# Output projection of a decoder layer: seven block products in place of eight for six heads and 1024 columns, with x and the deeper weight ring moved

## The chip, the cores and the metric

The kernel runs on one NeuronCore of one Trainium2 chip. The metric is the device time of one execution in microseconds; the median of 3 runs is 1096.73 us (1096.45 to 1097.01). The engines are named TensorE (PE; PEld for its weight loads), VectorE (DVE), ScalarE (ACT), GpSimd (POOL) and SyncE (SP, which only issues DMAs here).

## The reference, cut to what matters

One layer of a hybrid decoder: 256 tokens, width 2048, everything in float32. The change is in one matrix product, that of the mixed heads with `w_out`, between the attention and the residual:

```python
h = rms_norm(x, ln_mix_pre[l])
proj = h @ w_in[l]
...
attn = moba_attention(q.reshape(shp), k.reshape(shp), v.reshape(shp), rel_bias)
ssm = mamba2_mixer(z, xbc, dt_raw, ...)
mixed = jnp.concatenate([attn, ssm], axis=-1) @ w_out[l]
x = x + rms_norm(mixed, ln_mix_post[l])
h = rms_norm(x, ln_ffn_pre[l])
u = causal_depthwise_conv(h @ w_ffn_up[l], ffn_conv_w[l], ffn_conv_b[l])
gate, up = jnp.split(u, [FFN_HIDDEN], axis=-1)
f = (jax.nn.gelu(gate, approximate=True) * up) @ w_ffn_down[l]
x = x + rms_norm(f, ln_ffn_post[l])
```

`attn` has 8 heads of 128 columns, `ssm` 1024 columns; so `w_out` is 2048 x 2048.

## The kernel before

**Products in three matmuls.** Both operands of a large product are split into a rounded value and a remainder (`whi` and `wlo` for weights, two parts of each activation). A product is high by high, high by low and low by high, three matmuls into one accumulator in PSUM. `rows_part` (L312 to L319) does that for one unit of weights and one half of the tokens: the activations are the stationary side, 512 columns of weights move.

**Units and the ring.** Weights come as units of 128 x 1024 float32 (512 KB), in the order of the list given to `Weights`. For each unit SP issues a DMA into `raw` (L85), ScalarE casts it to `whi` (L86) and VectorE subtracts to get `wlo` (L87). `take()` hands the next finished unit to TensorE's code; `tick()`, called behind the matmuls of each unit, fetches one unit more and runs what `defer(n, ...)` has put off by n ticks. There are 4 buffers of `raw` and 4 of `whi` and `wlo`, so unit n + 4 is cast when unit n has been multiplied. `deepen` (L75) adds three buffers to `whi` and `wlo` from a pool of its own, and lets three ticks fetch a second unit. Each engine runs its instructions in a fixed order, and a waiting instruction holds all that stand behind it on its engine.

**The output projection.** A unit here is 256 rows of `w_out` by 512 columns, so it takes 2 halves of tokens x 2 blocks of rows x 3 = 12 matmuls. Chunk c is columns 512 c to 512 c + 511. `mT` holds the operand, transposed: blocks 0 to 7 are the heads, 8 to 15 the `ssm` part. Before the last attention head is finished the `ssm` rows of chunks 0 and 1 are multiplied (`rows_chunk(first[c], mT, lo, last=False)`, 8 units), then the heads' rows of both chunks (`hi`, 8 units), then chunks 2 and 3 with all rows. The last head's own steps (`logits`, `transposed`, `values`) are deferred by ticks into the first units.

**Behind each chunk.** `post(c)` (L847) squares and sums the chunk on ScalarE from PSUM, and VectorE multiplies it by `wpost` (the post norm's row, L850) into `mm` and that by `lnrow` (L842, `weighted`). `x_weighted` (L845) multiplies 512 columns of x by `lnrow`. Accumulators of a chunk come from a pool of four (`acc`), which the two first chunks fill.

**The loads.** When the attention's memory is free, GpSimd issues four DMAs of 1 MB: x by rows (`xt`, two of them, L821), then `wpost` (L826) and `lnrow` (L829), each a row repeated on all partitions; ScalarE multiplies `wpost` by -0.5 (L827). The ring is deepened at the same place (L823).

**Seven products for eight.** The down projection of the feed-forward part already forms products of 2 x 2 blocks with seven block products (a quad). Two units are loaded for it (`same` and `other`), two more are made of them (`two` and `more`): `quad_step` casts each on ScalarE (L137), forms the sums on VectorE (L141, L144, L145) and the remainders (L146). Four units carry 7 products of 3 matmuls (`product`, L1091); `quad_operands` forms the activations' sums, and `quad_sums` puts the four shared accumulators together with `fa`. That part runs with the deepened ring.

Of the kernel before, what the change touches and what calls it, by code (L numbers as in the profile page):

```python
# [19 lines left out]
P = 128  # L20
D = 2048
# [43 lines left out]
class Weights:  # L65
# [89 lines left out]
    def take(self):  # L155
        while not self.ready:
            self.fetch()
        return self.ready.pop(0)


@with_exitstack
def decoder_layer(ctx, tc, x, xT, win, wdt, wout, wup, wdown, relb, vec, cols, mconv, fconv,
# [20 lines left out]
    def tok(t):  # L183
        return slice(t * P, (t + 1) * P)
# [137 lines left out]
    def rows_chunk(pss, aT, kts, first=True, last=True, done=None, soon=None):  # L322
# [11 lines left out]
        if done:  # L334
            for t in range(NT):
                done(t, pss[t])

    def rows_to_tail(pss, aT, kts, first=True):
# [15 lines left out]
    def down_units(half):  # L354

        found, at = [], half * 44
        for what in 2 * ORDERS[half]:
# [3 lines left out]
            else:  # L361
                found += units(wdown, at, 1)
                at += 1
        return found

    ws = Weights(nc, wp, units(win, 0, 16, SHIFT) + units(win, 16, 16) + units(win, 32, 16, SHIFT)
                 + units(win, 48, 16) + units(win, 64, 24, SHIFT) + units(wout, 0, 32)
                 + [u for half in range(2) for u in units(wup, half * 88, 88) + down_units(half)])
# [42 lines left out]
    with ExitStack() as mctx:  # L411
        mx = mctx.enter_context(tc.tile_pool(name="mx", bufs=1))
        mT = mx.tile([P, KT, 2, S], F32R, name="mT")

        with ExitStack() as actx:
# [369 lines left out]
            def values(h, pT):  # L785
                po = psum("pav")
                nc.tensor.matmul(po[:, :S], v[:, 0, tok(h)], pT[:, :S], start=True, stop=False)
                nc.tensor.matmul(po[:, :P], v[:, 1, tok(h)], pT[:, S:], start=False, stop=True)
                split_evac(mT, h, slice(0, S), po[:, S - 1::-1])

            def head(h):
# [26 lines left out]
        mm = pers.tile([P, NT, D], F32, name="mm", tag="mm", bufs=1)  # L818
        xt = pers.tile([P, NT, D], F32, name="xt", tag="xt", bufs=1)
        for t in range(NT):  # L820
            aux(out=xt[:, t, :], in_=x[0, tok(t), :])  # L821
# [25 lines left out]
        def post(c):  # L847
            def fn(t, ps):
                square_sum(ss[0][t][:, c:c + 1], ps)
                nc.vector.tensor_tensor(mm[:, t, chunk(c)], ps, wpost[:, chunk(c)], op=ALU.mult)  # L850
                weighted(t, c)
                if (t, c) == (1, 2):
                    x_weighted(t, c)
            return fn
# [41 lines left out]


        for i, (t, c) in enumerate(((0, 0), (1, 0), (0, 1), (1, 1), (0, 2), (1, 3))):
# [168 lines left out]

    def blocks(ap):
        return ap.rearrange("p (b c) -> p b c", c=P)

    g8 = [None]

    def quad_operands(k, cg, cu):
# [9 lines left out]
        nc.vector.tensor_tensor(v[:, 2:4], blocks(cg), blocks(cu), op=ALU.mult)  # L1083
        nc.vector.tensor_tensor(v[:, 4:8:2], v[:, 0:2], v[:, 3::-3], op=ALU.subtract)
        nc.vector.tensor_tensor(v[:, 5], v[:, 4], v[:, 1], op=ALU.subtract)
        nc.vector.tensor_tensor(v[:, 7], v[:, 2], v[:, 5], op=ALU.add)
        src, hi, lo = g8[0][:, P:], gx[:, j, 0, :], gx[:, j, 1, :]
        nc.scalar.copy(hi, src)
        nc.vector.tensor_tensor(lo, src, f32(hi), op=ALU.subtract)

    def product(ps, j, block, w, h, first, last):  # L1091

        a, b = (gx[:, j, c, :][:, tok(block)] for c in range(2))
        s = chunk(h)
        nc.tensor.matmul(ps, a, w[0][:, s], start=first, stop=False)  # L1095
        nc.tensor.matmul(ps, a, w[1][:, s], start=False, stop=False)  # L1096
        end[0] = nc.tensor.matmul(ps, b, w[0][:, s], start=False, stop=last).ins  # L1097

    def quad_sums(half, c, p1, p6, p7, q5):
# [3 lines left out]
        if half == 0:  # L1103
            nc.scalar.copy(f[0][0], p1)
            tt(f[1][0], p6, f[0][0], op=ALU.add)
            tt(f[0][1], p7, f[1][0], op=ALU.add)
            tt(f[1][1], q5, f[0][1], op=ALU.subtract)
            tt(f[1][0], q5, f[1][0], op=ALU.subtract)
            return
# [286 lines left out]
```

## Time and profile before

| what | value |
|---|---|
| median of 3 runs | 1096.73 us |
| the profiled execution, its own time | 1097.02 us |
| its span, first to last instruction | 1095.2 us |
| mean granted clock of TensorE | 0.999 |
| busy: TensorE, VectorE, ScalarE, GpSimd | 99%, 81%, 57%, 1% |
| HBM read, written | 214.44 MB, 2.11 MB |
| output projection's matmuls on TensorE | 277.4 to 368 us |

A row of a group reads: line, engine, operation, output and inputs (buffer numbers left out), shapes and count; then busy us and mean ns of one; then idle time ahead of it and what ended it. A row of a time line starts with its start in us from the span's start and its length; two rows that follow overlap somewhat, since operations are pipelined, so the distance of starts is what an engine needs for one. A row of waits is engine and line, the one waited for, then us in total, times, and the longest.

### The profile page before, as it was taken

Reading aid. Unit: us, or ns where it says so; the run is one execution under the profiler, and the core shown is the slowest. Engines: PE = TensorE matmul, PEld = TensorE weight load, DVE = VectorE, ACT = ScalarE, POOL = GpSimd, SP = SyncE. Lnnn points to the kernel's source line nnn. Section 1 sums busy time; section 2 is a strip of 40 time slices with the busy share of each in tenths; the row PEclk is TensorE's granted clock in tenths of the full one; section 3 lists DMA queues with packets and bytes.
Section 4 is the critical chain, followed back from the end, with each engine's and each line's share of the span. In section 5 each row is a group of like instructions: output and inputs, shape, how many; then the busy total and the mean of one; then the engine's idle time right before and its main releaser. Section 6 shows DMA issues by size and latency. Waiting matters only on the chain.

```text
span 1095.2 us, 15949 instructions
## 1 busy us (share of the span) xinstructions
PE 1089.5 (99%) x5858; PEld 936.1 (85%) x5858; DVE 885.4 (81%) x1422; ACT 622.8 (57%) x945; POOL 14.5 (1%) x24
## 2 busy tenths in 40 slices
PE   9999999999999999999999999999999999999998
PEld 7888888888888998888888888888888888888887
DVE  6689976766568699888878999978888787888987
ACT  6666544644455486655555564646556555565552
POOL 0000000000000000000000000000000000000000
PEclk9999999999999999999999999999999999999999
DMA  9858544554687276656665476675566665656562
GB/s 308 301 174 269 191 154 152 177 180 166 182 320 252 76 254 212 208 183 192 190 191 191 135 232 190 215 245 186 187 189 193 189 192 193 189 178 217 185 219 88
DMA packets 61646, 217.59 MB, mean 199 GB/s; under 512 B 7104, under 2 KB 8912, under 8 KB 60928
## 3 DMA queue, kind: packets, MB, share of 16 engines
q1 hardware_dynamic: 59616, 207.53, 58.5%
q0 software_dynamic: 1664, 8.59, 2.1%
q8 instruction: 46, 0.75, 0.3%
q10 hardware_dynamic: 288, 0.46, 0.1%
q14 instruction: 32, 0.26, 0.1%
HBM read 214.44 MB, written 2.11 MB: 198 GB/s over the span
## 4 chain that ended last, share of the span: by engine, by line
PE 99%; DMA 0%; SPq 0%; ACT 0%; DVE 0%; issue 0%
PE pa L253 37%; PE pa L254 19%; PE pa L317 5%; PE pa L319 5%; PE pa L318 5%; PE ph L318 4%; PE ph L317 4%; PE ph L319 4%; PE pa L1096 1%; PE pa L1097 1%; PE pa L1095 1%; PE pab L253 1%; PE ph L1096 1%; PE ph L1097 1%; PE ph L1095 1%; PE pa L262 1%
## 5 line engine op out<-in xcount | busy, mean ns | idle before, releaser
L86 ACT CAST whi<-raw 128x1024 fp32r<-128x1024 f32 (+2 forms) x353 | 365.2, 1038 | 323.0 <-PE pa L253 186.6
L87 DVE TENSOR_TENSOR wlo<-raw,whi 128x1024 fp32r<-128x1024 f32 (+2 forms) x353 | 424.7, 1208 | 141.6 <-ACT whi L86 133.6
L253 PE MATMUL pa<-h,whi 128*128 128x512 f32 x1360 | 471.7, 394 | 0.0
L254 PE MATMUL pa<-h,wlo 128*128 128x256 f32 x1360 | 379.2, 279 | 0.0
L253 PEld LDWEIGHTS pa<-h,whi 128*128 128x128 f32 x1360 | 255.4, 188 | 57.5
L254 PEld LDWEIGHTS pa<-h,wlo 128*128 128x128 f32 x1360 | 255.3, 188 | 0.0
L253 PE MATMUL pa<-hT,whi 128*128 128x512 f32 x384 | 137.0, 398 | 0.0
L254 PE MATMUL pa<-hT,wlo 128*128 128x256 f32 x384 | 107.2, 280 | 0.0
L253 PEld LDWEIGHTS pa<-hT,whi 128*128 128x128 f32 x384 | 72.1, 188 | 15.8 <-issue 0.2
L1034 DVE SCALAR_TENSOR_TENSOR cfc<-cfu,fcv,cfc 128x255 f32<-128x255 f32 (+1 forms) x176 | 83.4, 479 | 2.1 <-ACT cfc L1032 0.6
L317 PE MATMUL ph<-whi,gT 128*128 128x512 f32 x190 | 73.9, 389 | 0.0
L319 PE MATMUL ph<-whi,gT 128*128 128x512 f32 x190 | 73.9, 389 | 0.0
L318 PE MATMUL ph<-wlo,gT 128*128 128x512 f32 x190 | 73.9, 389 | 0.0
L254 PEld LDWEIGHTS pa<-hT,wlo 128*128 128x128 f32 x384 | 72.2, 188 | 0.4 <-issue 0.2
L137 ACT CAST whi<-ts 128x1024 fp32r<-128x1024 f32 x36 | 37.3, 1049 | 31.3 <-DVE ts L145 16.8
L1032 ACT ACTIVATE cfc<-cfu,fcv 128x256 f32<-128x256 f32 x88 | 52.2, 598 | 3.7 <-DVE cfu L1031 3.7
L317 PE MATMUL pa<-whi,hT 128*128 128x512 f32 x128 | 51.1, 399 | 0.0
L317 PE MATMUL pa<-whi,mT 128*128 128x512 f32 x128 | 50.3, 393 | 0.0
L319 PE MATMUL pa<-whi,hT 128*128 128x512 f32 x128 | 50.1, 391 | 0.0
L318 PE MATMUL pa<-wlo,hT 128*128 128x512 f32 x128 | 50.0, 391 | 0.0
L318 PE MATMUL pa<-wlo,mT 128*128 128x512 f32 x128 | 50.0, 390 | 0.0
L319 PE MATMUL pa<-whi,mT 128*128 128x512 f32 x128 | 49.9, 390 | 0.0
(306 smaller groups left out, 1391.2 us busy)
## 6 DMA issues: line engine op xcount, KB each, us to landing
raw<-in_wup_dram SPq DMA_DIRECT2D x176, 512.0 KB, 3.5
raw<-in_wdown_dram SPq DMA_DIRECT2D x88, 512.0 KB, 3.9
raw<-in_win_dram SPq DMA_DIRECT2D x85, 512.0 KB, 3.6
raw<-in_wout_dram SPq DMA_DIRECT2D x32, 512.0 KB, 4.0
xsq<-in_x_dram SPq DMA_DIRECT2D x4, 512.0 KB, 8.6
rows<-acd POOLq DMA_DIRECT2D x4, 512.0 KB, 8.0
xt<-in_x_dram POOLq DMA_DIRECT2D x2, 1024.0 KB, 7.2
xr<-in_xT_dram SPq DMA_DIRECT2D x6, 256.0 KB, 6.0
```

The costliest lines, as they stand in the source:

```text
L86: nc.scalar.copy(hi[:, s], raw[:, s])
L87: return lambda: nc.vector.tensor_tensor(lo[:, s], raw[:, s], f32(hi[:, s]), op=ALU.subtract)
L137: nc.scalar.copy(hi[:, :n], raw[:, :n])
L253: nc.tensor.matmul(ps, w[0][:, s], both, start=(k == 0), stop=False)
L254: end[0] = nc.tensor.matmul(ps[:, c], w[1][:, s], hi, start=False, stop=(k == KT - 1)).ins
L317: nc.tensor.matmul(ps, a, w[0][:, s], start=(first and j == 0), stop=False)
L318: nc.tensor.matmul(ps, a, w[1][:, s], start=False, stop=False)
L319: end[0] = nc.tensor.matmul(ps, b, w[0][:, s], start=False, stop=(last and j == 1)).ins
L1032: nc.scalar.activation(c, u, AF.Identity, scale=wv[:, 2:3], bias=wv[:, 3:4])
L1034: nc.vector.scalar_tensor_tensor(c[:, sh:], u[:, :S - sh], wv[:, 2 - sh:3 - sh], c[:, sh:], op0=ALU.mult, op1=ALU.add)
L1095: nc.tensor.matmul(ps, a, w[0][:, s], start=first, stop=False)
L1096: nc.tensor.matmul(ps, a, w[1][:, s], start=False, stop=False)
```

## The change

For heads 0 to 5 (three pairs) and chunks 0 and 1 together, the output projection is formed with quads. The string `OUTER` sets the order: a digit is a plain unit of that chunk, Q a quad of four units. The first six plain units run as before while the last head is finished; then come Q 1 Q 1 Q 0 1. Heads 6 and 7 and the `ssm` rows stay plain.

```diff
+OUTER = "000011Q1Q1Q01"
+OQ = OUTER.count("Q")
...
+class Spare:
+    def tile(self, *args, **kwargs):
+        self.n += 1
+        return self.places[self.n % len(self.places)]
...
                 split_evac(mT, h, slice(0, S), po[:, S - 1::-1])
+                if h < 2 * OQ:
+                    out_operands(h, po[:, S - 1::-1])
...
+            def out_operands(h, a):
+                j, odd = divmod(h, 2)
+                if not odd:
+                    og[0] = ax.tile([P, 8 * P], F32, name="og", tag="og", bufs=1)
+                    nc.scalar.copy(blocks(og[0])[:, 1::-1], blocks(a))
+                    return
+                nc.scalar.copy(blocks(og[0])[:, 2:4], blocks(a))
+                block_sums(blocks(og[0]))
+                split(oq[:, j, 0, :], oq[:, j, 1, :], og[0][:, 4 * P:])
...
+            mm = pers.tile([P, NT, D], F32, name="mm", tag="mm", bufs=1)
+            ws.sums = Spare([mm[:, t, UE:] for t in range(NT)])
             first = [chunk_psums() for _ in range(2)]
-            for c in range(2):
-                rows_chunk(first[c], mT, lo, last=False)
+            taken = [list(lo) + list(hi[OQ:]) for _ in range(2)]
+            for what in OUTER[:6]:
+                c = int(what)
+                rows_step(first[c], mT, taken[c].pop(0), first=len(taken[c]) == 4 - OQ + 3)
...
-        for t in range(NT):
-            aux(out=xt[:, t, :], in_=x[0, tok(t), :])
-        ws.deepen(ctx.enter_context(tc.tile_pool(name="wq", bufs=1, side="right")))
+        defer(21, ws.deepen, ctx.enter_context(tc.tile_pool(name="wq", bufs=1, side="right")))
...
         def post(c):
             def fn(t, ps):
+                m = mm[:, t, chunk(c)]
+                if c < 2:
+                    nc.vector.tensor_tensor(m, ps, m, op=ALU.add)
+                    ps = m
                 square_sum(ss[0][t][:, c:c + 1], ps)
...
+                if c < 2:
+                    defer(3 + c + t, rest)
...
+        def out_pair():
+            once = [psum("pm7") for _ in range(4)]
+            p1, p7, q5, p6 = once
+            j = 0
+            for what in OUTER[6:]:
+                if what == "Q":
+                    for items in (((p1, 0, 0), (first[1][0], 6, 1)), ((first[0][0], 1, 0),),
+                                  ((q5, 3, 0), (p7, 5, 1)), ((p6, 4, 0), (first[0][1], 2, 1))):
+                        w = ws.take()
+                        for ps, block, h in items:
+                            mine = any(ps is z for z in once)
+                            out_product(ps, j, block, w, h, mine and j == 0,
+                                        mine and j == OQ - 1)
+                        tick()
+                    j += 1
+                    if j == OQ:
+                        with tc.issue_after(end[0]):
+                            for t in range(NT):
+                                aux(out=xt[:, t, :], in_=x[0, tok(t), :])
+                        first_sums([[mm[:, t, chunk(n)] for t in range(NT)] for n in range(2)],
+                                   p1, p6, p7, q5)
...
-            defer(9 + i, x_weighted, t, c)
-        for c in range(2):
-            rows_chunk(first[c], mT, hi, first=False, soon=post(c))
+            defer(19 + i, x_weighted, t, c)
+        out_pair()
```

`rows_step` is one plain unit as `rows_chunk` has it; `block_sums`, `split`, `product_of` and `first_sums` are the bodies of what the down projection did in place (`first_sums` is a copy and four sums or differences of 512 columns). Sums of weights go to the second half of `mm`, which nothing uses yet. Four accumulators more (`pm7`) hold the shared products; `post` adds them to chunks 0 and 1 ahead of the squares.

How this moves instructions is shown at three places. First GpSimd, where the loads stand. Before:

```order
L194 TENSOR_TENSOR rsy<-rsa,mhalf 128x1 x4
L821 DMA xt<-in_x_dram 128x2048 x2
L826 DMA wpost<-in_vec_dram 128x2048
L829 DMA lnrow<-in_vec_dram 128x2048
L219 TENSOR_TENSOR lsy<-lsa,mhalf 128x1 x2
```

In the change, with the semaphores that each waits for:

```order
L207 TENSOR_TENSOR rsy<-rsa,mhalf 128x1 [waits DVE_49] x4
L909 DMA wpost<-in_vec_dram 128x2048 [waits DVE_49,DMAHW0_49,PE_49,Activation_49]
L912 DMA lnrow<-in_vec_dram 128x2048
L1020 DMA xt<-in_x_dram 128x2048 [waits DMASW5_49]
L1020 DMA xt<-in_x_dram 128x2048 [waits DMASW1_49]
L232 TENSOR_TENSOR lsy<-lsa,mhalf 128x1 [waits DVE_49] x2
```

The two loads of x stand behind the two rows of the norms instead of ahead of them; they wait for two DMAs of GpSimd's own queue (the earlier loads of the bias and of `rows`) and for no other engine.

Second VectorE, behind the values of the last head (`mT<-pav`). Numbers are those of the buffers; before, each `raw` is one unit:

```order
L87 TENSOR_TENSOR wlo_2977<-raw_2975,whi_2976 128x1024
L241 TENSOR_TENSOR mT_98<-pav_2981,mT_98 128x256
L87 TENSOR_TENSOR wlo_3069<-raw_3067,whi_3068 128x1024
L87 TENSOR_TENSOR wlo_3000<-raw_2998,whi_2999 128x1024
L87 TENSOR_TENSOR wlo_3075<-raw_3073,whi_3074 128x1024
```

In the change; raw_3062 and raw_3074 are the two blocks of the second quad, raw_3124 and raw_3136 those of the third (units 16 and 17), whi_3052 is unit 10 and whi_3114 unit 15:

```order
L254 TENSOR_TENSOR mT_98<-pav_3006,mT_98 128x256
L146 TENSOR_TENSOR mm_2862<-mm_2862,raw_3062 128x512
L89 TENSOR_TENSOR wlo_3053<-raw_3051,whi_3052 128x1024
L148 TENSOR_TENSOR wlo_3061<-raw_3062,whi_3060 128x1024
L148 TENSOR_TENSOR wlo_3073<-raw_3074,whi_3072 128x512
L147 TENSOR_TENSOR mm_2862<-mm_2862,raw_3074 128x512
L148 TENSOR_TENSOR wlo_3086<-mm_2862,whi_3085 128x1024
L148 TENSOR_TENSOR wlo_3104<-mm_2862,whi_3103 128x1024
L143 TENSOR_TENSOR mm_2862<-raw_3124,raw_3136 128x1024
L89 TENSOR_TENSOR wlo_3115<-raw_3113,whi_3114 128x1024
L148 TENSOR_TENSOR wlo_3123<-raw_3124,whi_3122 128x1024
L148 TENSOR_TENSOR wlo_3135<-raw_3136,whi_3134 128x512
```

Where one remainder followed the other in the order of the units, the sums for a quad now stand between them, and the sum of the third quad's two blocks (L143) stands ahead of the remainder of unit 15.

Third VectorE at the end of chunks 0 and 1. Before:

```order
L87 TENSOR_TENSOR wlo_3117<-raw_3115,whi_3116 128x1024
L845 TENSOR_TENSOR xl0_3044<-xt_3025,lnrow_3041 128x512
L87 TENSOR_TENSOR wlo_3123<-raw_3121,whi_3122 128x1024
L850 TENSOR_TENSOR mm_3024<-pa_2837,wpost_3038 128x512
L850 TENSOR_TENSOR mm_3024<-pa_2838,wpost_3038 128x512
L842 TENSOR_TENSOR ml0_3043<-mm_3024,lnrow_3041 128x512
```

In the change, from the last remainder of the third quad (unit 19) on; `pm7` are the shared products, `pa` the chunks' own accumulators:

```order
L148 TENSOR_TENSOR wlo_3166<-mm_2862,whi_3165 128x1024
L89 TENSOR_TENSOR wlo_3177<-raw_3175,whi_3176 128x1024
L89 TENSOR_TENSOR wlo_3186<-raw_3184,whi_3185 128x1024
L89 TENSOR_TENSOR wlo_3198<-raw_3196,whi_3197 128x1024
L89 TENSOR_TENSOR wlo_3210<-raw_3208,whi_3209 128x1024
L388 TENSOR_TENSOR mm_2862<-pm7_3044,mm_2862 128x512
L928 TENSOR_TENSOR xl0_3030<-xt_3013,lnrow_3027 128x512
L389 TENSOR_TENSOR mm_2862<-pm7_3042,mm_2862 128x512
L934 TENSOR_TENSOR mm_2862<-pa_2863,mm_2862 128x512
```

The chunks' accumulators are now emptied by the additions of `post` (L934) behind the sums of the shared products; the products with `wpost` and `lnrow` follow later.

More of the change, by code (lines that the diff above doesn't have):

```diff
@@ L336, in rows_chunk, with rows_step, blocks, block_sums @@
                 done(t, pss[t])
+    def rows_step(pss, aT, k, first=False, last=False, soon=None):
+        w = ws.take()
+        for t in range(NT):
+            rows_part(pss[t], w, aT, k, t, first, last)
+        if soon:
+            for t in range(NT):
+                soon(t, pss[t])
+        tick()
+    def blocks(ap):
+        return ap.rearrange("p (b c) -> p b c", c=P)
+    def block_sums(v):
+        nc.vector.tensor_tensor(v[:, 4:8:2], v[:, 0:2], v[:, 3::-3], op=ALU.subtract)
+        nc.vector.tensor_tensor(v[:, 5], v[:, 4], v[:, 1], op=ALU.subtract)
+        nc.vector.tensor_tensor(v[:, 7], v[:, 2], v[:, 5], op=ALU.add)
+    def split(hi, lo, src):
+        nc.scalar.copy(hi, src)
+        nc.vector.tensor_tensor(lo, src, f32(hi), op=ALU.subtract)
+    def product_of(ps, a, b, w, h, first, last):
+        s = chunk(h)
+        nc.tensor.matmul(ps, a, w[0][:, s], start=first, stop=False)
+        nc.tensor.matmul(ps, a, w[1][:, s], start=False, stop=False)
+        end[0] = nc.tensor.matmul(ps, b, w[0][:, s], start=False, stop=last).ins
+    def first_sums(f, p1, p6, p7, q5):
+        tt = nc.vector.tensor_tensor
+        nc.scalar.copy(f[0][0], p1)
+        tt(f[1][0], p6, f[0][0], op=ALU.add)
+        tt(f[0][1], p7, f[1][0], op=ALU.add)
+        tt(f[1][1], q5, f[0][1], op=ALU.subtract)
+        tt(f[1][0], q5, f[1][0], op=ALU.subtract)
     def rows_to_tail(pss, aT, kts, first=True):
@@ L364, in down_units, with out_units @@
         return found
+    def out_units():
+        found, at = [], 0
+        for what in OUTER:
+            if what == "Q":
+                found += [("same", wout[at]), ("other", wout[at + 1]), ("two",), ("more",)]
+                at += 2
+            else:
+                found += units(wout, at, 1)
+                at += 1
+        return found + units(wout, at, 16)
     ws = Weights(nc, wp, units(win, 0, 16, SHIFT) + units(win, 16, 16) + units(win, 32, 16, SHIFT)
-                 + units(win, 48, 16) + units(win, 64, 24, SHIFT) + units(wout, 0, 32)
+                 + units(win, 48, 16) + units(win, 64, 24, SHIFT) + out_units()
                  + [u for half in range(2) for u in units(wup, half * 88, 88) + down_units(half)])
@@ L1083, in quad_operands @@
         nc.vector.tensor_tensor(v[:, 2:4], blocks(cg), blocks(cu), op=ALU.mult)
[L1084 to L1089, printed above, removed]
-    def product(ps, j, block, w, h, first, last):
[L1093 to L1097, printed above, removed]
+        block_sums(v)
+        split(gx[:, j, 0, :], gx[:, j, 1, :], g8[0][:, P:])
+    def product(ps, j, block, w, h, first, last):
+        product_of(ps, *(gx[:, j, c, :][:, tok(block)] for c in range(2)), w, h, first, last)
     def quad_sums(half, c, p1, p6, p7, q5):
@@ L1338 @@
     ssm, att = [4, 5, 6, 7], [0, 1, 2, 3]
[L1339 to L1340 removed]
+    head, quads = [], iter(att)
+    plain = [iter(ssm + att[OQ:]) for _ in range(2)]
+    for what in OUTER:
+        if what == "Q":
+            k = next(quads)
+            (b11, b21), (b12, b22) = (o[n, k].reshape(P, 2, 512).swapaxes(0, 1) for n in range(2))
+            head += [np.concatenate(z, axis=1) for z in ((b11, b22), (b21, b12))]
+        else:
+            head.append(o[int(what), next(plain[int(what)])])
+    wout = np.concatenate([np.stack(head), o[2, ssm + att], o[3, ssm + att]])
     up = cols(w_up).reshape(2, NF, 2, P, UE)
```

41 lines of the change are left out of this document (27 added, 14 removed).

## The prediction

> **What bounds the kernel now.** I read the page first, then the waits of TensorE, then time lines and DMA issues of the stretch that the change rewrites. The page's busy line and the engine line of its chain:
>
> ```profile
> PE 1089.5 (99%) x5858; PEld 936.1 (85%) x5858; DVE 885.4 (81%) x1422; ACT 622.8 (57%) x945; POOL 14.5 (1%) x24
> PE 99%; DMA 0%; SPq 0%; ACT 0%; DVE 0%; issue 0%
> ```
>
> TensorE is busy in 99% of the span and is 99% of the chain. All its waits in the whole run:
>
> ```profile
> PE idle L385 <- DVE junk L382: 1.1, 1, 1.1
> PE pab L254 <- DVE wlo L87: 0.2, 1, 0.2
> PE pab L253 <- ACT whi L86: 0.2, 1, 0.2
> ```
>
> So it waits 1.5 us, all of it at the start. A removed matmul therefore saves its own time, and any new wait costs its full length. In stretches of 10 us (columns: TensorE, weight loads, VectorE, ScalarE, GpSimd, clock, DMA share, GB/s), before, in and behind the loads of x and of the two norm rows:
>
> ```profile
> 270.00:280.00 10.00, 10.00 (x57) 8.70 (x56) 6.78 (x15) 4.93 (x10) 0.00 (x0) 1.00 0.51 148
> 300.00:310.00 10.00, 10.00 (x46) 8.29 (x45) 4.42 (x4) 3.45 (x4) 0.00 (x0) 1.00 1.01 418
> 320.00:330.00 10.00, 10.00 (x45) 8.28 (x45) 9.85 (x13) 7.60 (x14) 0.00 (x0) 1.00 0.73 214
> ```
>
> The clock is full throughout. From 300 to 310 the DMA engines are full (1.01); VectorE idles there and catches up at 320 (9.85 of 10).
>
> **What is removed.** TensorE's time line in the output projection:
>
> ```profile
> 296.42 0.48 PE L317 MATMUL pa<-whi,mT 128*128 128x512 f32 x1
> 299.47 0.39 PE L318 MATMUL pa<-wlo,mT 128*128 128x512 f32 x1
> 302.19 0.39 PE L318 MATMUL pa<-wlo,mT 128*128 128x512 f32 x1
> ```
>
> Between the last two rows lie 12 matmuls (one unit): 2.72 / 12 = 0.227 us each from start to start. A quad has 7 products of 3 matmuls in place of 8: 3 fewer, for three quads 9. 9 x 0.227 = **2.04 us removed**. The first row is where the first quad will start, since the six units and the last head ahead of it are multiplied as before.
>
> **What is added, and who does it.** I number the units of the output projection from 0. In the change 0 to 5 are plain, 6 to 9, 11 to 14 and 16 to 19 are the quads, 10, 15, 20 and 21 plain, and chunk 2 begins at 22. Durations, of the same operations in the down projection and elsewhere:
>
> ```profile
> L87 DVE TENSOR_TENSOR wlo<-raw,whi 128x1024 fp32r<-128x1024 f32 x345 | 420.4, 1223 | 139.7 <-ACT whi L86 131.7 <-PE pab L254 1.3
> L141 DVE TENSOR_TENSOR ts<-raw 128x1024 f32<-128x1024 f32 x18 | 21.9, 1219 | 2.2 <-DMA raw<-in_wdown_dram 2.1
> L144 DVE TENSOR_TENSOR ts<-ts,raw 128x512 f32<-128x512 f32 x18 | 12.3, 684 | 0.1
> L146 DVE TENSOR_TENSOR wlo<-raw,whi 128x512 fp32r<-128x512 f32 x18 | 12.3, 685 | 0.3 <-ACT whi L137 0.3
> ```
>
> A quad gives VectorE three remainders of 1.22, one of 0.69, one broadcast sum of 1.22 and two sums of 0.68: 6.9 us, beside 21 x 0.227 = 4.8 us of TensorE. In before two units need 2.4 us of VectorE beside 5.4. VectorE is the slower one inside a quad, with a ring of four units ahead instead of seven. Its time line, with ScalarE's casts, around the loads in before:
>
> ```profile
> 297.17 1.23 DVE L87 TENSOR_TENSOR wlo<-raw,whi 128x1024 fp32r<-128x1024 f32 x1 [1.85 <-ACT whi L86]
> 298.31 0.42 DVE L241 TENSOR_TENSOR mT<-pav,mT 128x256 fp32r<-128x256 f32 x1
> 300.52 2.36 DVE L87 TENSOR_TENSOR wlo<-raw,whi 128x1024 fp32r<-128x1024 f32 x2 [1.79 <-ACT whi L86]
> 321.29 1.28 DVE L850 TENSOR_TENSOR mm<-pa,wpost 128x512 f32<-128x512 f32 x2
> ...
> 306.85 2.00 ACT L86 CAST whi<-raw 128x1024 fp32r<-128x1024 f32 x2 [5.41 <-DMA raw<-in_wout_dram]
> 310.61 1.05 ACT L86 CAST whi<-raw 128x1024 fp32r<-128x1024 f32 x1 [1.76 <-DMA raw<-in_wout_dram]
> 315.04 1.05 ACT L86 CAST whi<-raw 128x1024 fp32r<-128x1024 f32 x1 [3.38 <-DMA raw<-in_wout_dram]
> ```
>
> Two remainders back to back take 2.36, two 512-wide operations 1.28: pitches of 1.14 and 0.60. The casts show weights landing late. The DMA issues of 298 to 299, 301 to 303 and 303 to 305 (last number: us to landing; an issue on an edge is in both), then of 283 to 286, ahead of the loads:
>
> ```profile
> raw<-in_wout_dram SPq DMA_DIRECT2D x1, 512.0 KB, 8.4
> ...
> raw<-in_wout_dram SPq DMA_DIRECT2D x2, 512.0 KB, 10.4
> ...
> raw<-in_wout_dram SPq DMA_DIRECT2D x1, 512.0 KB, 12.0
> ...
> raw<-in_wout_dram SPq DMA_DIRECT2D x2, 512.0 KB, 3.5
> ```
>
> Three weight blocks issued beside the 4 MB of loads took 8.4, 8.8 (2 x 10.4 - 12.0) and 12.0 us, in place of 3.5. In before the ring covers it.
>
> **The wait that I expect.** GpSimd's order has the four loads at the same place as before, released by the last head's values; only the norm rows now come ahead of x. `issue_after` names a matmul, but nothing in the order shows GpSimd waiting for the products. So the 4 MB fall on the quads. VectorE's order puts the broadcast sum of the third quad, which needs the blocks of units 16 and 17, ahead of the remainder of unit 15. If block 17 is late, unit 15 stands behind it, though its own block landed long before.
>
> Step by step. The head's values evacuate at 298.31 on VectorE as in before; then come a sum (0.60) and the remainders of units 10 and 11, from about 299.25, 1.14 apart. When they end, at about 300.5 and 301.65, SP issues blocks 16 and 17. Block 17's landing is bounded by rows: the 8.8 us of the block issued at 301.7, also second in its queue, gives 310.5; unit 16 taking 8.4, and 17 landing as far behind it as the casts 310.61 and 306.85 stand apart (3.76), gives 312.6; with 3.5, as without loads, 305.2. I take 311.5, between the first two, since the loads are queued as before.
>
> TensorE needs the remainder of unit 15 for that unit's second matmul. From 296.42 there are 21 + 12 + 21 matmuls (12.24) to 308.66, and one more: 308.89. The sum takes 1.14 and the remainder 1.22 to its end: 311.5 + 2.36 = 313.86. **Wait 4.97 us**.
>
> Behind it VectorE is the slower one up to chunk 2, whose first accumulator is free only when VectorE has added its old content (L934). From the start of unit 15's remainder it runs eight remainders (8 x 1.14), eight operations of 0.60 and that addition (0.68): 14.6 us. TensorE has 1.22 of waiting and 56 matmuls: 13.9. **0.7 us more**.
>
> Edits at nothing. The operands of the heads add about 1.7 us of VectorE per two heads (a 256-wide and two 128-wide sums, a remainder); VectorE is at 6.78 of 10 from 270 to 280 and nothing waits; without that cover, up to 1.7 us each. ScalarE's product with wpost stands between the casts of units 13 and 14 and waits for the load:
>
> ```profile
> L821 POOL DMA_DIRECT2D xt<-in_x_dram x2: 543/572/601, 297.2 to 297.8; - x2
> xt<-in_x_dram POOLq DMA_DIRECT2D x2, 1024.0 KB, 7.2
> ...
> xt<-in_x_dram POOLq DMA_DIRECT2D x1, 1024.0 KB, 8.8
> wpost<-in_vec_dram POOLq DMA_DIRECT2D x1, 1024.0 KB, 12.0
> ...
> 317.27 1.91 ACT L827 ACTIVATE wpost<-wpost 128x2048 f32<-128x2048 f32 x1
> ```
>
> The first load landed in 2 x 7.2 - 8.8 = 5.6 us, at 302.8; wpost has that place now, and 1.91 and a cast of 1.05 later unit 14 is ready at 305.8 and its remainder at 307.0; 49 matmuls from 296.42 it is needed, at 307.5: 0.5 to spare, and what the load is later than that is added. x lands third and fourth instead of first and second. The third load of before took 12.0, so x's first rows land near 310; their first products (L928) stand eight operations behind unit 15's remainder, near 318 with the wait and 313 without it. SP issues 32 blocks in both kernels, in the order of the units. The later ring, and the sums and products of `post` moved into chunk 2, cost nothing as far as I can bound it: 11 remainders (12.5) and 14 operations of 0.60 (8.4) beside 8 x 2.72 = 21.8 us of TensorE, with two to three units of ring between them. None of these can gain either: TensorE waits for nothing that they could shorten.
>
> **Sum.** -2.04 + 4.97 + 0.7 = +3.6 us. The profiled execution is 1097.02 us (span 1095.2 and 1.8 around it), 0.3 over the median: it would be 1100.6, the median **1100.3**. (Lines of the changed kernel are meant where the text names L143, L331, L928 and L934.) With landing at 310.5 the median is 1099.3, at 312.6 it is 1101.4: the likeliest case's own range.
>
> **Rivals.** A difference below 0.2% (2.2 us) can't be told from none here.
>
> *Blocks land in time* (ends not slower): block 17 takes 3.5 us. The sum then starts when VectorE is free, near 306.9, the wait for unit 15 is 0.4, the 0.7 stays: -2.04 + 1.1 gives 1095.8. For it: in the first 3 us of the loads SP has nothing outstanding. Against it: the three rows above. It decides where block 17 lands before 306.5.
>
> *TensorE never waits*: also VectorE's lag is hidden. -2.04 gives 1094.7, within 0.2%. For it: no wait in the down projection's quads; against it, those have seven units of ring and no 4 MB.
>
> *The clock falls in the wait*: the 16 first matmuls of the run, and 12 of their form at its end:
>
> ```profile
> 1.09 3.42 PE L385 MATMUL idle<-junk 128*128 128x256 bf16 x16 [1.09 <-DVE junk L382]
> L1181 PE MATMUL idle<-cst 128*128 128x256 bf16 x12 | 1.5, 273 | 0.0
> ```
>
> Per matmul 0.214 against 0.125: after an idle stretch TensorE is slow for 3.4 us at least, a loss of 3.42 x (1 - 0.125 / 0.214) = 1.4 us. If a wait of 5 us does the same, 1.4 less the 0.7 that VectorE then no longer trails: 1101.0 to 1101.7. Against it: no idle stretch inside the run shows it. The Trainium skill (TensorE: Matmul & The Clock Gate, Part 1) says that about 3.4 us of idling bring half rate, until about 3.4 us of work: by that rule this case would be the likeliest.
>
> *x is held back after all*, until the last product, as the code reads: then only 2 MB meet the quads, but VectorE's order has two products with x ahead of the remainder of unit 19, which would wait for each other. So I give it nothing.
>
> **How the numbers follow.** Forecast 0.52, clock 0.10: slower by over 0.2%, 0.62. Blocks in time 0.20: same. TensorE never waiting 0.18: same 0.12 and, by the spread of a median, faster 0.06. The range leaves out that last case: 1095.6 (just below blocks in time) to 1102.4 (the clock's upper case, 0.7 over its estimate for what else may slip).
>
> **What would show it.** In the profile after: 9 matmuls fewer; TensorE waiting for VectorE at L331, once, for 4 to 6 us, near 309 to 314, with VectorE's L143 idle ahead of it for a DMA of in_wout_dram; a short wait on L934. The forecast is wrong if TensorE shows no wait of over 1 us there, or if block 17 lands before 307.

## The result, and the profile after

The changed kernel takes 1104.37 us (median of 6 runs, 1103.68 to 1104.72), the kernel before 1096.81 (6 runs): a ratio of 1.0068 (95% interval 1.0055 to 1.0081). That is 7.6 us slower where 3.6 was forecast. The profiled execution took 1103.81 us with a span of 1102.0, 6.8 more than before.

The page's busy line and the engine line of its chain, after:

```profile
PE 1090.4 (99%) x5849; PEld 936.2 (85%) x5849; DVE 905.6 (82%) x1457; ACT 631.4 (57%) x961; POOL 14.0 (1%) x24
PE 96%; DVE 2%; DMA 1%; issue 1%; ACT 0%; POOL 0%; DVEq 0%; ACTq 0%
```

TensorE has the nine matmuls fewer (5849 for 5858) and is yet busy for longer, and VectorE and a DMA have come into the chain. TensorE's waits in the whole run (us in total, times, longest):

```profile
PE pa L331 <- DVE wlo L89: 5.7, 1, 5.7
PE idle L452 <- DVE junk L449: 1.1, 1, 1.1
PE pa L330 <- DVE mm L934: 0.3, 1, 0.3
PE pyt L817 <- DVE xs L810: 0.3, 1, 0.3
```

Two of the three new waits were forecast: one long one on a remainder, a short one on L934. The third, at L817, was not, and it lies at 188 us, some 90 us ahead of the projection. TensorE's time line around the long wait and at the start of chunk 2 (start, length; in brackets the idle time ahead):

```profile
296.50 0.48 PE L380 MATMUL pm<-whi,mT 128*128 128x512 f32 x1
...
308.84 0.39 PE L330 MATMUL pa<-whi,mT 128*128 128x512 f32 x1
314.90 0.79 PE L331 MATMUL pa<-wlo,mT 128*128 128x512 f32 x1 [5.67 <-DVE wlo L89]
315.49 0.63 PE L332 MATMUL pa<-whi,mT 128*128 128x512 f32 x1
...
319.74 0.39 PE L380 MATMUL pm<-whi,mT 128*128 128x512 f32 x1
...
329.77 0.39 PE L332 MATMUL pa<-whi,mT 128*128 128x512 f32 x1
330.50 0.47 PE L330 MATMUL pa<-whi,mT 128*128 128x512 f32 x1 [0.34 <-DVE mm L934]
```

From 308.84 the next matmul should start 0.227 later, at 309.07; it starts at 314.90, 5.83 us late. Then 11 matmuls, the rest of unit 15, take 314.90 to 319.74: 4.84 us, 0.44 each. At 0.227 they would take 2.50, so 2.34 us are lost without any wait. In the stretches of 6 us, the clock (third number from the end) shows why:

```profile
308.00:314.00 6.00, 1.23 (x6) 0.69 (x4) 1.51 (x2) 1.84 (x3) 0.00 (x0) 0.91 0.84 345
314.00:320.00 6.00, 5.10 (x13) 4.01 (x14) 6.00 (x8) 0.87 (x1) 0.00 (x0) 0.53 0.57 167
```

VectorE and ScalarE at the wait:

```profile
312.49 1.23 DVE L143 TENSOR_TENSOR mm<-raw 128x1024 f32<-128x1024 f32 x1 [5.64 <-DMA raw<-in_wout_dram]
313.63 1.22 DVE L89 TENSOR_TENSOR wlo<-raw,whi 128x1024 fp32r<-128x1024 f32 x1
...
308.64 1.05 ACT L139 CAST whi<-raw 128x1024 fp32r<-128x1024 f32 x1 [1.90 <-DMA raw<-in_wout_dram]
312.46 0.62 ACT L139 CAST whi<-raw 128x512 fp32r<-128x512 f32 x1 [2.78 <-DMA raw<-in_wout_dram]
```

This is the chain that was forecast: the sum of the third quad (L143) stands idle for block 17, which lands at 312.46, and behind it stands unit 15's remainder, whose own block had landed long before.

**The account of the profiled execution**, from rows: -2.04 (nine matmuls), +5.83 (the wait), +2.34 (the slow matmuls), +0.50 (330.50 instead of 330.00), +0.08 more at that restart (its matmul has a pitch of 0.31), +0.08 (the first quad starts at 296.50 instead of 296.42): 6.8, as measured. The median moved 0.77 us more than the profiled executions did (before, the profiled one lay 0.21 above its median, after 0.56 below).

### The profile page after: what moved, and what is told of

Same layout as the page of the kernel before. It is cut to its first block, busy times and chain, and to the rows that moved or that the text cites. A ratio compares the mean times of both kernels' runs of the same rounds, so it can differ in the third digit from the quotient of the medians.

```text
span 1102.0 us, 15985 instructions
## 1 busy us (share of the span) xinstructions
PE 1090.4 (99%) x5849; PEld 936.2 (85%) x5849; DVE 905.6 (82%) x1457; ACT 631.4 (57%) x961; POOL 14.0 (1%) x24
## 4 chain that ended last, share of the span: by engine, by line
PE 96%; DVE 2%; DMA 1%; issue 1%; ACT 0%; POOL 0%; DVEq 0%; ACTq 0%
PE pa L266 36%; PE pa L267 19%; PE pa L331 4%; PE pa L330 4%; PE pa L332 4%; PE ph L331 4%; PE ph L332 4%; PE ph L330 4%; PE pa L382 2%; PE pa L381 2%; PE pa L380 1%; PE pab L266 1%; PE ph L381 1%; PE ph L382 1%; PE ph L380 1%; DVE wlo L89 1%
## 5 line engine op out<-in xcount | busy, mean ns | idle before, releaser
L88 ACT CAST whi<-raw 128x1024 fp32r<-128x1024 f32 (+2 forms) x347 | 358.9, 1039 | 297.3 <-PE pa L266 183.3
L89 DVE TENSOR_TENSOR wlo<-raw,whi 128x1024 fp32r<-128x1024 f32 (+2 forms) x347 | 416.8, 1207 | 117.8 <-ACT whi L88 111.2
L139 ACT CAST whi<-raw 128x1024 fp32r<-128x1024 f32 (+1 forms) x42 | 35.0, 837 | 34.0 <-PE ph L332 12.1
L148 DVE TENSOR_TENSOR wlo<-ts,whi 128x1024 fp32r<-128x1024 f32 x36 | 43.7, 1222 | 8.7 <-ACT whi L139 8.4
L331 PE MATMUL pa<-wlo,mT 128*128 128x512 f32 x104 | 41.6, 400 | 5.7 <-DVE wlo L89 5.7
```

The source lines that it names most:

```text
L88: nc.scalar.copy(hi[:, s], raw[:, s])
L89: return lambda: nc.vector.tensor_tensor(lo[:, s], raw[:, s], f32(hi[:, s]), op=ALU.subtract)
L139: nc.scalar.copy(hi[:, :n], raw[:, :n])
L148: return lambda: nc.vector.tensor_tensor(lo[:, :n], raw[:, :n], f32(hi[:, :n]), op=ALU.subtract)
```

## The experiments

Ten kernels ran, in three groups (1 to 4, 5 to 8, 9 and 10). Each ratio is to the kernel before as it ran in the same group; its medians there were 1096.94, 1097.11 and 1097.25 us, so a difference of a few tenths between kernels of different groups says nothing. Line numbers shift by a few lines between kernels; each fence's operations are named.

**1. The sum behind the remainders.** In `quad_step`, the broadcast sum of a quad is issued on VectorE behind the last remainder (that of the quad's first block, and so behind unit 15's too):

```diff
-            add(*two, raw[:, None, 512:].to_broadcast([P, 2, 512]), op=ALU.add)
+            with self.tc.issue_after(self.last):
+                add(*two, raw[:, None, 512:].to_broadcast([P, 2, 512]), op=ALU.add)
...
+            self.last = nc.vector.tensor_tensor(lo[:, :n], raw[:, :n], f32(hi[:, :n]),
+                                                op=ALU.subtract).ins
```

> Edit: on VectorE the broadcast sum of a quad's two blocks is ordered behind the remainder of the unit ahead and of the quad's first block, so that unit 15's remainder no longer stands behind block 17. The loads stay as they are. Theory (one late block holds back a remainder that was ready, and the clock falls in the idling): no wait at unit 15; block 17 still lands near 312.5, so the sum ends near 313.6 and TensorE waits about 2 us in pieces of about 1 at units 17 and 18, too short for the clock to fall, and about 0.6 us behind them: -2.0 + 2.2 + 0.6 gives about 1097.6 (1096.5 to 1098.5). Rival (the block itself, not the order, is what TensorE lacks; it would merely stop later at the same block): the wait of 5 us is found again at unit 16 or 17, with the fall of the clock, and the time is 1102 or more.

1099.89 us, ratio 1.0027 (1.0017 to 1.0038): 4.5 us less than the changed kernel, yet 2.3 more than expected. TensorE's time line (L386 needs the remainder):

```profile
313.33 0.50 PE L385 MATMUL pa<-whi,mT 128*128 128x512 f32 x1
314.53 0.50 PE L386 MATMUL pa<-wlo,mT 128*128 128x512 f32 x1 [0.70 <-DVE wlo L152]
...
315.08 0.50 PE L385 MATMUL pm<-whi,oq 128*128 128x512 f32 x1
316.34 0.50 PE L386 MATMUL pm<-wlo,oq 128*128 128x512 f32 x1 [0.76 <-DVE wlo L152]
```

and the stretch of the stops with the one behind it:

```profile
314.00:317.00 3.00, 1.71 (x6) 1.06 (x7) 3.00 (x5) 1.54 (x3) 0.00 (x0) 1.00 0.40 71
317.00:320.60 3.60, 3.60 (x10) 2.27 (x9) 3.60 (x5) 3.60 (x4) 0.00 (x0) 0.53 0.77 259
```

Block 17 is as late as before, and the wait for unit 15 is gone: the order made it. What is left are two stops at units 17 and 18, 1.2 us from start to start instead of 0.227, 2.0 us together, just as expected. Not expected: the clock falls behind these two, and the stretch of 3.6 us shows 0.53; the matmuls there lose 1.8 us against a distance of 0.227 from start to start. With the 0.47 us that run 5 traces to the ssm, that is about the difference.

**2. x held back.** The two loads of x wait for the third quad's last remainder, so only 2 MB meet the quads:

```diff
-                        with tc.issue_after(end[0]):
-                            for t in range(NT):
-                                aux(out=xt[:, t, :], in_=x[0, tok(t), :])
+                        for t in range(NT):
+                            nc.gpsimd.tensor_copy(xt[:, t, :1], f32(w[1][:, :1]))
+                            aux(out=xt[:, t, :], in_=x[0, tok(t), :])
```

> Edit: GpSimd's two loads of x wait, by a copy of one column, for the last remainder of the third quad; only the 2 MB of the two norm rows then meet the quads. VectorE's order stays as in the changed kernel. Theory (the four loads make block 17 late): with half the bytes block 17 lands near 308; its sum and unit 15's remainder end near 310.4, a wait of 1 to 1.5 us, and the clock stays up; with 0.6 behind it -2.0 + 1.3 + 0.6 gives about 1096.7 (1095.7 to 1098). Rival (VectorE's own work or the casts make the sum late, not the loads): the wait stays over 4 us and the time over 1101.

1105.28 us, ratio 1.0076 (1.0063 to 1.0089). TensorE's waits of over 0.6 us in the projection, and VectorE's time line:

```profile
PE pa L330 <- DVE mm L934: 5.9, 1, 5.9
...
PE pa L331 <- DVE wlo L89: 0.7, 1, 0.7
```

```profile
308.02 1.23 DVE L143 TENSOR_TENSOR mm<-raw 128x1024 f32<-128x1024 f32 x1 [0.91 <-DMA raw<-in_wout_dram]
...
327.66 0.69 DVE L928 TENSOR_TENSOR xl<-xt,lnrow 128x512 f32<-128x512 f32 x1 [5.35 <-DMA xt<-in_x_dram]
...
328.87 0.68 DVE L934 TENSOR_TENSOR mm<-pa,mm 128x512 f32<-128x512 f32 x1
```

Half of the theory holds: with 2 MB less, block 17 is there by 308.02 instead of 312.49, and the wait at unit 15 falls from 5.7 to 0.7. So the loads make the block late. But the same trap opens further on: a product of x (L928) stands in VectorE's order ahead of the addition that empties the accumulator which chunk 2 needs (L934), and now it is x that is late. Behind that wait of 5.9 us the clock falls too (0.51 from 330 to 336). VectorE's order is not quite that of the changed kernel: two products of x that ran there at 318.84, ahead of unit 19's remainder, now come behind L934. The prediction had named such an order as its reason against the rival "x is held back"; the expectation of this run overlooked it.

**3. Both.** The edits of 1 and 2 together.

> Edit: both of the two others, the sum behind the remainders and x held back until the third quad's last remainder. Theory: no wait over 0.5 us is left in the quads, the 2.0 us of the nine matmuls are seen, less at most 0.6 where VectorE lags at chunk 2's accumulators: 1094.7 to 1095.5. Rival (something else in the change costs time as well, such as the later ring, the products of x that come later, or the work moved into chunk 2): 1096.5 or more, with a wait that shows where.

1104.72 us, ratio 1.0069 (1.0056 to 1.0083). The quads have no wait of over 0.2 us any more, and all is lost at L940, the L934 of this kernel, and in the slow matmuls behind it (0.44 us apart from 330.48 to 335.74):

```profile
PE pa L335 <- DVE mm L940: 6.7, 1, 6.7
```

**4. TensorE kept busy in the wait.** In the changed kernel, 48 matmuls of zeros that add nothing stand ahead of unit 15:

```diff
+            still = junk[:, :S // 2].bitcast(BF16)
+            nc.gpsimd.memset(still, 0.0)
...
+                    if j == 2:
+                        for _ in range(FILL):
+                            nc.tensor.matmul(first[c][0][:, :S], still[:, :P], still, start=False,
+                                             stop=False)
```

> Edit: 48 matmuls of zeros (128x256, bf16) that add nothing are put on TensorE ahead of unit 15, where it idles; at 0.125 us each they fill 6.0 us, about the wait. Nothing else is changed. Theory (11 matmuls at 0.427 us behind the wait are the clock, which falls because TensorE idles): the matmuls behind the wait keep 0.227 us, and 2.35 us less than the changed kernel are needed up to chunk 2, of which VectorE, that has some 2 us of idling up to chunk 2's accumulators, lets through about 2: about 1102.3 (1101.8 to 1103). Rival (those matmuls are slow for another reason, their weights or the DMA traffic): they stay at 0.427 and the time at 1104 to 1105.

1103.07 us, ratio 1.0056 (1.0043 to 1.0068), 1.3 us less than the changed kernel. TensorE's time line and stretches:

```profile
308.98 5.41 PE L1031 MATMUL pa<-junk 128*128 128x256 bf16 x48
...
314.96 0.50 PE L332 MATMUL pa<-wlo,mT 128*128 128x512 f32 x1 [0.34 <-DVE wlo L90]
...
322.58 0.50 PE L382 MATMUL pm<-wlo,oq 128*128 128x512 f32 x1 [1.16 <-DVE wlo L149]
```

```profile
308.00:314.00 6.00, 6.00 (x52) 5.12 (x51) 1.46 (x2) 1.79 (x3) 0.00 (x0) 1.00 0.82 340
314.00:320.00 6.00, 5.66 (x27) 4.44 (x26) 6.00 (x8) 1.84 (x2) 0.00 (x0) 1.00 0.50 165
```

The block is as late, unit 15's second matmul, which needs the remainder, starts at the same time (314.96 for 314.90), and the clock stays at 1.00: the idling is what made it fall. Of the 2.34 us saved, a stop at 322.58 (1.3 us late) takes back 1.3. TensorE waits there for unit 19's remainder; VectorE's time line:

```profile
318.90 2.49 DVE L929 TENSOR_TENSOR xl<-xt,lnrow 128x512 f32<-128x512 f32 x4
321.31 1.22 DVE L149 TENSOR_TENSOR wlo<-mm,whi 128x1024 fp32r<-128x1024 f32 x1
```

The order on VectorE has moved with the edit, against what the expectation says: four products of x stand ahead of this remainder, where the changed kernel has two. Its cast was done at 320.14, so the two more, at 0.60 each, account for about 1.2 of the 1.3 us.

**5. Both, and the products of x behind the additions.**

```diff
         def x_weighted(t, c):
-            nc.vector.tensor_tensor(xl[t][c], xt[:, t, chunk(c)], lnrow[:, chunk(c)], op=ALU.mult)
+            with tc.issue_after(added[0]):
+                nc.vector.tensor_tensor(xl[t][c], xt[:, t, chunk(c)], lnrow[:, chunk(c)],
+                                        op=ALU.mult)
...
-                    nc.vector.tensor_tensor(m, ps, m, op=ALU.add)
+                    added[0] = nc.vector.tensor_tensor(m, ps, m, op=ALU.add).ins
```

> Edit: the sum behind the remainders and x held back, as in the run of both, and in addition VectorE's products of x with lnrow ordered behind the additions that empty the accumulators of chunks 0 and 1. Theory (in the run of both, TensorE waited 6.7 us only because one such product, waiting for x, stood ahead of those additions): no wait over 0.5 us from the quads to chunk 2, the clock stays full, and the 2.0 us of nine matmuls are seen: 1094.8 (1094.4 to 1096). Rival (x's 2 MB, now falling on chunk 2, make the weights of chunk 2 late whatever VectorE's order): a wait of 1 us or more for the remainders of units 24 to 26, and 1097 or more.

1096.96 us, ratio 0.9997 (0.9988 to 1.0006): the 7.8 us that run 3 lost are gone, so the order of the products of x did it, but of the 2.0 us of nine matmuls nothing is seen. The rival doesn't explain it: no unit of chunk 2 waits for its weights. TensorE's waits of this run that lie behind its start are two:

```profile
PE pyt L823 <- DVE xs L816: 0.3, 1, 0.3
...
PE pa L335 <- ACT whi L89: 0.2, 1, 0.2
```

Starts of matmuls tell the rest. The first quad starts at 297.21 instead of 296.42: 0.33 of that is there from the first weights on (pyt, the transposes of the ssm's first half, starts at 188.37 instead of 188.04) and goes back and forth between executions; 0.47 come between that and the second half's (211.74 instead of 210.94). And from the first quad to the end of chunk 3 (the first transposes of the normed rows, 364.57) TensorE takes 67.36 us instead of 68.29: 0.93 less and not 2.04. The other 1.1 lie in late starts just behind 306.8 (0.19), 316.2 (0.63) and 323.2 (0.36, the start of chunk 2, which waits for the addition), mostly too short to be shown as waits, behind VectorE and ScalarE.

**6. The loads spread.** As 5, but wpost's load goes as in the changed kernel, and those of lnrow and x wait for the remainders of units 11, 16 and 19 (one each):

```diff
+LATE = (5, 9, 12)
...
+                        n += 1
+                        if n in LATE:
+                            dst, src = late.pop(0)
+                            nc.gpsimd.tensor_copy(dst[:, :1], f32(w[1][:, :1]))
+                            aux(out=dst, in_=src)
                         tick()
```

> Edit: as the run with both and the products late, but the four loads of 1 MB are spread: wpost's goes as in the changed kernel, lnrow's, and the two of x, each wait for one remainder, those of units 11, 16 and 19. Theory: each load then meets about two blocks of weights instead of all four meeting the same three; no wait over 0.5 us anywhere in the projection, 1094.8 (1094.4 to 1095.6), at or below the run with both and the products late. Rival (the loads cost the same wherever they lie in the quads, since VectorE has no slack there): block 16 or 17 is late again by 1 us or more, and 1096 or more.

1097.48 us, ratio 1.0003 (0.9994 to 1.0012). Block 17 lands at 309.81, which is early enough, and the late starts of run 5 are there too: 0.4 behind 306.4, 0.6 behind 315.9, and 0.85 behind 322.9, where chunk 2 waits for the addition.

Spreading is no better than holding x back; neither removes what is left.

**7. The moves without the quads.** The kernel before, with x's loads behind the norm rows' and the later ring:

```diff
-        for t in range(NT):
-            aux(out=xt[:, t, :], in_=x[0, tok(t), :])
...
-        ws.deepen(ctx.enter_context(tc.tile_pool(name="wq", bufs=1, side="right")))
+        defer(13, ws.deepen, ctx.enter_context(tc.tile_pool(name="wq", bufs=1, side="right")))
...
+        for t in range(NT):
+            aux(out=xt[:, t, :], in_=x[0, tok(t), :])
...
-            defer(9 + i, x_weighted, t, c)
+            defer(11 + i, x_weighted, t, c)
```

> Edit: the kernel before, with only the two moves of the change: x's loads behind those of the two norm rows, and the deeper ring (with the products of x two ticks later) 13 ticks later. No quads. Theory (the loss needs the quads: VectorE's order and its longer work): a late block delays only its own unit, and a ring of four has some 10 us of multiplication ahead of it; block issued near 301 lands near 312.5 as in the changed kernel, just about when it is wanted: 1096.8, at most 1 us more. Rival (the later ring and the later x are themselves what costs, with or without quads): 1100 or more, with a wait of 3 us or more.

1096.98 us, ratio 0.9998 (0.9990 to 1.0007). TensorE's waits show nothing behind the first weights:

```profile
PE idle L385 <- DVE junk L382: 1.1, 1, 1.1
PE pab L254 <- DVE wlo L87: 0.4, 1, 0.4
```

The blocks are late here too, the casts behind the loads wait for them until 311.51 and 314.95, and TensorE doesn't wait for the casts. Without the quads the moves cost nothing.

**8. The ring deepened at once.**

```diff
-        defer(21, ws.deepen, ctx.enter_context(tc.tile_pool(name="wq", bufs=1, side="right")))
+        ws.deepen(ctx.enter_context(tc.tile_pool(name="wq", bufs=1, side="right")))
```

> Edit: in the changed kernel the ring is deepened at once, as in the kernel before, instead of 21 ticks later. Theory (block 17 is late because it is issued when the loads are already queued): with three buffers more of whi and wlo, casts run ahead and blocks 16 and 17 are issued some 3 us earlier, about when the loads are issued; block 17 lands 2 to 4 us earlier, the wait falls from 5.8 to 2 to 4 us, and the time to 1099.5 to 1102.5. Rival (a ring that was deep in time covers the loads entirely, as in the kernel before): no wait, 1095 to 1096. Other rival (the ring has no part in it): 1104 to 1105.

1106.78 us, ratio 1.0086 (1.0072 to 1.0100), outside all three expectations. VectorE's time line:

```profile
312.18 1.23 DVE L143 TENSOR_TENSOR mm<-raw 128x1024 f32<-128x1024 f32 x1 [1.38 <-DMA raw<-in_wout_dram]
...
330.12 1.28 DVE L934 TENSOR_TENSOR mm<-pa,mm 128x512 f32<-128x512 f32 x2
```

and TensorE's, whose matmul ahead of this one starts at 326.64:

```profile
330.94 0.76 PE L330 MATMUL pa<-whi,mT 128*128 128x512 f32 x1 [3.91 <-ACT whi L88]
```

Block 17 lands at 312.18, no earlier in any way that counts. The remainder of unit 15 now stands ahead of the sum (it ran at 306.46), as in run 1, and stops of up to 1.2 us follow in the quads, 4.9 us together. The loss at chunk 2 is new: its first matmul starts 4.1 us late, and the 12 from it on are 0.44 us apart. The profile names a cast, but by the order of the casts that of chunk 2's first unit was done at 319.6, while the first L934 ends at about 330.8. With the deeper ring, VectorE's order takes seven remainders of plain units between the last sum of the quads and L934, where the changed kernel has four, and they wait for their blocks. In the changed kernel the delay of the ring is worth about 2 us. In the quads the clock stays at 1.00 in spite of the stops; the last section comes back to that.

**9. Two orders smoothed.** As 5, with the product by -0.5 (wpost) moved on ScalarE behind the casts of the third quad, and on VectorE the second of the two sums for a quad's last unit ahead of the remainder before it:

```diff
-        nc.scalar.mul(wpost, wpost, -0.5)
...
+                        with tc.issue_after(ws.cast):
+                            nc.scalar.mul(wpost, wpost, -0.5)
...
+            with self.tc.issue_after(self.sum if kind == "two" else self.cast):
+                self.last = nc.vector.tensor_tensor(lo[:, :n], raw[:, :n], f32(hi[:, :n]),
+                                                    op=ALU.subtract).ins
```

> Edit: the run with both and the products late, and two more orders: ScalarE's product with wpost stands behind the casts of the third quad instead of between those of units 13 and 14, and on VectorE the second sum of a quad's last unit stands ahead of the remainder of the unit before it. Theory (of the 2.0 us of nine matmuls that run gave back 1.1 us in small stops of TensorE in the projection, near 306.8, 316.2 and 323.2 us, behind VectorE and ScalarE): the first two go, 0.8 us, and the third, 0.36, may stay: 1096.1 (1095.7 to 1096.5). Rival (VectorE's amount of work sets it, not its order): the stops come back later, at chunk 2's accumulators, and the time stays at 1096.9.

1095.91 us, ratio 0.9987 (0.9978 to 0.9996). All three late starts are gone, the third too. The starts of the first quad and of the transposes behind chunk 3, in this run, and the transposes' in the kernel before, whose first quad starts at 296.42:

```profile
297.21 0.48 PE L386 MATMUL pm<-whi,mT 128*128 128x512 f32 x1
...
363.48 1.03 PE L984 MATMUL pxt<-cst,ml 128*128 128x128 f32 x8
```

```profile
364.71 1.03 PE L881 MATMUL pxt<-cst,ml 128*128 128x128 f32 x8
```

That is 66.27 us for 68.29, 2.02 less than before. The two orders were changed together, so which of them removed which late start isn't shown.

**10. And the gate's product first.** As 9, and in the ssm's first half the remainders that VectorE had ahead of the gate's second product (xs) are emitted behind it:

```diff
...
+            if kept and i >= n - kept:
+                ws.kept = ws.kept or []
             tick()
         if done:
             for t in range(NT):
                 done(t, pss[t])
+        if kept:
+            rests, ws.kept = ws.kept, None
+            with tc.issue_after(ws.gate):
+                for rest in rests:
+                    rest()
```

> Edit: as the smoothed run, and in addition, in the ssm's gate of the first half, the remainders that VectorE has put ahead of the second gate product (xs) since the heads' operands were added are held behind it. Theory (the changed kernel and all with quads wait 0.3 us at L817, pyt, and are 0.47 us later from there on, because of such a remainder): 0.47 us less than the smoothed run, 1095.6 (1095.2 to 1096.1), no wait at pyt. Rival (the held remainders are then late for their own unit): as much or more is lost just behind it.

1095.17 us, ratio 0.9981 (0.9972 to 0.9990), against 1097.25 for the kernel before: 2.1 us faster, what nine matmuls are worth, and clear of noise (its runs lie between 1094.61 and 1095.63, those of the kernel before at 1096.67 or more). TensorE's waits and the engine line of the page's chain:

```profile
PE idle L472 <- DVE junk L469: 1.1, 1, 1.1
PE pab L278 <- ACT whi L91: 0.5, 2, 0.3
PE pab L279 <- DVE wlo L92: 0.2, 1, 0.2
```

```profile
PE 99%; DMA 0%; SPq 0%; ACT 0%; DVE 0%; issue 0%
```

The waits are again those of the start alone, and the chain is TensorE's. From pyt to pyt it is 187.89 to 210.79, 22.90 us as before. This version beats both kernels, by 0.2% and 0.8%.

## Why the prediction was wrong, point by point

- **Nine matmuls, -2.04 us**: right. Nothing shows of it until every new stop is gone; then runs 9 and 10 show 2.02 us in the projection and 2.1 in the median.
- **The wait at unit 15, 4.97 us**: right in mechanism and place (run 1 removes it by the order, run 2 all but 0.7 of it by the loads), too small by 0.86. The term that was mis-sized is the landing: block 17 came at 312.46, the upper bound of 312.6, and not at the 311.5 that was chosen. It was issued between 301 and 302, as forecast, and took longer than the 8.8 us of the row of before; the issue of that microsecond in the changed kernel (last number, us to landing):

```profile
raw<-in_wout_dram SPq DMA_DIRECT2D x1, 512.0 KB, 10.7
```

- **The clock, given 0.10**: this step failed, by 2.34 us. The forecast's sum put the slow matmuls behind the wait at nothing; run 4 shows that they are the clock's. The reason against the fall was that no idle stretch inside the run shows it; there was none to show it, since TensorE never idled in before. That is absence of evidence, and the only idle stretch that there was, the start, spoke for the fall (by the distance of its matmuls, 0.214 us for 0.125; the clock column reads 1.00 there). The price was too low as well: 1.4 us less 0.7 assumed 3.42 us of slow time, and there were 4.84. The rule of the Trainium skill (TensorE: Matmul & The Clock Gate, Part 1), half rate after an idle window of about 3.4 us, came out here: the clock fell to 0.50 some 3.6 us behind the stop (in other runs 2.4 to 5.3 us, see the last section). Its 3.4 us of work until full rate were 4.84 here.
- **VectorE's lag, 0.7**: right in kind and about in size. It shows as 0.5 in the changed kernel, where the slow matmuls gave VectorE time, and as 1.1 in run 5; most of the 1.3 in run 4 are two products of x that moved. Its cause isn't only the amount of work, as the prediction's sum of operations had it: the two orders changed in run 9 remove it.
- **The heads' operands at nothing**: wrong by 0.47. The cover was read from 270 to 280 us alone, but the first pair of heads has its values at 159 and 174, and VectorE's order in the ssm behind that changed: the changed kernel and runs 1, 5, 6 and 9 take 23.37 or 23.38 us from pyt to pyt instead of 22.90, and holding the remainders behind the gate's product (run 10) brings 22.90 back. In the changed kernel a remainder starts on VectorE at 186.55, ahead of the product xs at 187.89; in the kernel before xs starts at 187.38 and the remainder behind it, at 187.78. Without quads (run 7) the old order and 22.90 are there. That it was the operands that changed this order is inferred; what was shown is the order's price. In the changed kernel's span it is hidden by an earlier start of 0.38.
- **The ring and the moves at nothing**: right as far as run 7 shows it, without quads; with them the delay of the ring even saves about 2 us (run 8).
- **Rivals**: *blocks in time* and *TensorE never waits* needed block 17 by 306.5. Its landing was 6 us later. *x is held back* was rightly given nothing: the loads of the changed kernel go at once. Run 2 shows that holding x back would cost as much, at L934 instead of at unit 15.

From forecast to result: 0.86 (landing) + 2.34 (clock) - 0.12 (lag, 0.58 for 0.7) + 0.08 (start) + 0.77 (medians against profiled executions) = 3.9 of the 4.0 us between +3.6 and +7.6. What made the changed kernel's runs spread over 1.0 us, and its profiled one the second lowest, stays open.

## What to carry to other kernels

A change that saves work on the bounding engine is worth that work only if each helper's queue still delivers in the order in which that engine asks: look for the one instruction that waits for something late and has something needed behind it, at every place where the order moved, and not only where the new work stands. Price a wait of TensorE with the slow matmuls behind it; several short stops close together can bring them too (run 1), though they need not (run 8). Where a trace has no example of a state, it is no evidence that the state can't occur.

## What was not expected of the hardware

The clock fell without one long idle stretch. In run 1, two stops of 1.0 us each within 3 us were followed by the stretch at 0.53; in run 4, two stops of 0.6 and 1.3 us that lay 7.6 us apart were not (1.00 in the rows above, and up to 332 as well). But that the stops lie close together doesn't decide it. In run 8, five stops of 0.4 to 1.2 us lie between 313 and 321, and the clock is 1.00 up to 329; a stretch of them:

```profile
314.00:317.00 3.00, 1.24 (x3) 0.48 (x3) 1.84 (x4) 3.00 (x4) 0.00 (x0) 1.00 0.46 128
```

TensorE is busy for 1.24 of these 3 us, less than the 1.71 in run 1. What makes the clock fall behind short stops stays open.

In the changed kernel the full clock was still granted for some 3.6 us after TensorE had stopped at about 309.2:

```profile
312.00:313.00 1.00, 0.00 (x0) 0.00 (x0) 0.51 (x1) 0.54 (x1) 0.00 (x0) 0.94 0.89 361
313.00:314.00 1.00, 0.00 (x0) 0.00 (x0) 1.00 (x2) 0.26 (x2) 0.00 (x0) 0.50 0.09 33
...
319.00:320.00 1.00, 1.00 (x5) 0.78 (x4) 1.00 (x2) 0.00 (x0) 0.00 (x0) 0.65 0.94 381
```

The full clock was back only near 319.7, after 4.8 us of slow work, 1.4 us more than the 3.4 of the start, by which the prediction had priced it. From the stop to the fall it took 5.2 and 5.3 us in runs 2 and 3 and 2.4 us in run 8, but in all four kernels the half clock then lasted 6.8 us (in run 1, 3.4 us). These times are read in rows of 0.1 us. The slow work is what is left of the 6.8 us when the wait ends.

And the weights' blocks did not share with GpSimd's loads from the moment of their issue. The queues of the changed kernel in the stretches 303 to 304 and 304 to 305 (packets, MB, share of 16 engines):

```profile
q0 software_dynamic: 50, 0.41, 96.9%
...
q0 software_dynamic: 44, 0.24, 57.0%
q1 hardware_dynamic: 41, 0.17, 40.7%
```

Blocks had been issued since 300, and up to 304 all data was GpSimd's, 2.0 MB, as much as the two norm rows; only then did the blocks get their part, 0.13 to 0.17 MB in a microsecond beside 0.24 to 0.29. That fits block 17's landing at 312.5 with 4 MB and at 308.0 with 2 MB (run 2). What the blocks wait for isn't shown; in the kernel before they got their part between 302 and 303 already, when GpSimd's queue had moved at most 1.4 MB.
